# Where 64 row multiplies of the last adaLN gate stand among the two products of an MLP

## The chip, the cores and the metric

The kernel runs on one core of a Trainium2 chip. The metric is the time of one execution on the device in microseconds (us), the median of several runs. A core has engines with a queue of instructions each, which they work off in order: TensorE (PE in the profile; PEld is its weight load), VectorE (DVE), ScalarE (ACT), GpSimd (POOL) and SyncE (SP). They wait for each other through semaphores. DMA transfers are issued from the queues of SP, ACT and POOL and run beside the engines.

## The reference

One decoder layer: attention beside a recurrence, then an MLP with squared ReLU. A conditioning vector c gives six adaLN vectors (shift, scale and gate of each half). Cut to what matters here:

```
c_act = silu(c)
mod = (c_act @ w_ada + b_ada).reshape(B, 6, D)
sh1, sc1, gt1, sh2, sc2, gt2 = [mod[:, j][:, None, :] for j in range(6)]
...
h = rmsnorm(x, g_norm_mlp) * (1.0 + sc2) + sh2
hid = square(relu(einsum('bsd,df->bsf', h, w_mlp_in)))
y = einsum('bsf,fd->bsd', hid, w_mlp_out)
x = x + gt2 * y
return rmsnorm(x, g_norm_final)
```

There are 512 tokens, D is 2048 and the MLP is 8192 wide. gt2, the last gate, is needed only where the MLP's second product is finished.

## The kernel before

All values are float32. Each factor of a product is split into a high and a low half of TensorE's reduced format (a rounded copy on ScalarE, the rest by a subtraction on VectorE, `low`, L122), and a product is three matmuls.

**The two products of the MLP** are computed by Strassen's scheme: 7 products of sums of blocks in place of 8. One *set* is what one step along the inner dimension costs: 7 products, 2 halves and 3 matmuls each, 42 matmuls of 128x256. `operands` (L1053) makes a set's weights: one load of 512 KB into `raw` (three buffers), sums on VectorE (L1060, L1067, L1068), two copies on ScalarE (L1066, L1072) and two subtractions on VectorE (L122). `strassen` (L1083) runs over the sets of a list, holds its 7 results in 7 of the 8 PSUM banks, and calls `tick()` after each set.

The first product (loop at L1217) has 15 such groups of 8 sets, g = 1 to 15. After a group `combine` (L1110) adds up the 7 banks: a copy on ScalarE (L1113), then seven steps on VectorE (L1114 to L1120). The next group takes the eighth bank first and then the banks as combine frees them. `keep_parts` (L928) then squares and splits the result, adds sums for the second product (L948), and stores them as *parts* and *sums*; `hold_parts` (L952) does so for the last two groups without storing them.

The second product (loop at L1257) goes through a list `parts` of 13 pieces of 8, 16 or 12 sets; piece i works on column block n. Where a block isn't finished in a piece, its 7 banks are stored to DRAM (`prodD`, POOL's queue) and fetched again later: five by `load_pre` (L1236) on POOL's queue into tiles of the tag `n` (five buffers), two more on ACT's queue, copied into the banks by ScalarE at L1090 and L1092. Piece 3 (block 3) has 16 sets; the piece behind it is the first that fetches. Pairs of stored parts are fetched by `load_pair` (L1136: three loads at L1141, two at L1144, on SP's queue) and split by `split_pair` (L1148), both at set numbers worked out beforehand. From its block's last piece on, a block is added up with the gate: the first time at piece 9.

**The row multiplies.** `ada_late(GT2)` (L1188) computes gt2: 64 rows, each a load of 256 KB of `w_adaT` on SP's queue (L1192), three rows ahead, and one multiply with accumulation on VectorE (L1203); after four rows two small steps (L1208, L1209) give one column of gt2. It is a generator in the lane `bg2`: it yields a number of sets, and `tick()` runs it on when so many have passed. `pace[0]` is that number (1.9, L1215). `ensure(GT2)` (L1276) runs what is left of it, before piece 9's combine.

**What sets the order.** A scheduler orders each engine's instructions when the kernel is built, by the program's order less an offset given by `high_priority` (operands 200, combine 330 instructions ahead), and by when it takes data to be there. `keep_in_program_order` ties an instruction behind the one traced just before it on its engine. The rows' loads are tied in this way, their multiplies are not.

Sets are numbered below as VectorE begins them (its L1060): 1 to 120 are the first product, 121 to 244 the second; piece 3 has the sets 145 to 160.

Of the kernel before, what the change touches and what calls it, by code (L numbers as in the profile page):

```python
# [39 lines left out]
SH1, SC1, GT1, SH2, SC2, GT2 = range(6)  # L40
# [24 lines left out]
def hybrid_layer_kernel(  # L65
# [32 lines left out]
    def T(tag, dt=F32, cols=None):  # L98
        return new(next(split_tag) if tag == "w4" else tag, dt, cols)

    def new(tag, dt=F32, cols=None):
        count[0] += 1
        pool, bufs = (sp, BUFS[tag]) if tag in BUFS else pools[tag][:2]
        return pool.tile([P, cols or COLS[tag]], dt, tag=tag, name=f"{tag}_{count[0]}", bufs=bufs)

    def bank(tag):
        count[0] += 1
        return pp.tile([P, S], F32, tag=tag, name=f"ps_{tag}_{count[0]}", bufs=PBUFS[tag])
# [5 lines left out]
    stt = nc.vector.scalar_tensor_tensor  # L114
# [33 lines left out]
    def col(base, j):  # L148
        return vec[:, base + j : base + j + 1]
# [23 lines left out]
    for i in range(2):  # L173
        v = slice(i * S, (i + 1) * S)
        ps = bank("mm")
# [7 lines left out]
    def mod(m, j):  # L183
        return mods[:, m * NK + j : m * NK + j + 1]
# [80 lines left out]
    def blk(o):  # L265
        return slice(o * P, (o + 1) * P)


    class Lane:
# [8 lines left out]
        def next(self):  # L278
            if not self.queue:
                return False  # L280
            try:
                self.wait += next(self.queue[0]) or 0.0
            except StopIteration:
                self.queue.pop(0)
            return True
# [13 lines left out]
    bg, bgl, bg2 = Lane(), Lane(), Lane()  # L299

    def tick(dt=1.0):
        for lane in (bg, bgl, bg2):
            lane.run(dt)
# [137 lines left out]
    for o in range(8):  # L441
        t = T("a")
# [266 lines left out]
    pace = [3.2]  # L709

    def ensure(m):
        while m not in ready:
            assert bg2.next()
# [339 lines left out]
    def operands(src):  # L1053

        with tc.high_priority(offset=SETW):

            r = T("raw")
            nc.sync.dma_start(r.rearrange("p (c f) -> p c f", c=2), src)
            t = T("ts")
            tt(  # L1060
                out=t[:, : 2 * HT].rearrange("p (a b) -> p a b", a=2),
                in0=r[:, HT : 3 * HT].rearrange("p (a b) -> p a b", a=2),
                in1=r[:, q_(0)].unsqueeze(1).broadcast_to([P, 2, HT]), op=ALU.add,
            )
            h, lo = T("w3", F32R), T("w3", F32R)
            act(h, r[:, HT:], AF.Copy)  # L1066
            tt(out=t[:, q_(2)], in0=t[:, q_(0)], in1=r[:, q_(2)], op=ALU.add)  # L1067
            tt(out=t[:, q_(3)], in0=t[:, q_(2)], in1=r[:, q_(3)], op=ALU.add)  # L1068
            low(lo, r[:, HT:], h)
            out = {n: (h[:, q_(i)], lo[:, q_(i)]) for i, n in enumerate(("11", "22", "21"))}  # L1070
            h, lo = T("w4", F32R), T("w4", F32R)
            act(h, t, AF.Copy)  # L1072
            low(lo, t, h)
            for i, n in enumerate(("t1", "t3", "t2", "t4")):
                out[n] = h[:, q_(i)], lo[:, q_(i)]
        return out
# [3 lines left out]

    loaded = [None]

    def strassen(src, acts, after=None, pre=None, before=None, js=range(8)):  # L1083

        bs = [bank(next(turn)) for _ in PRODUCTS]
        if pre:
            n, ts = pre
            with tc.high_priority(offset=SETE):
                for b, t in zip(bs, ts):
                    act(b, t, AF.Copy)  # L1090
                for b, t in zip(bs[5:], load_pre(n, (5, 6), nc.scalar)):
                    act(b, t, AF.Copy)  # L1092
        if before:
            loaded[0] = before()
        for j in js:
            w, a = operands(src(j)), acts(j)
            for b, (an, wn) in zip(bs, PRODUCTS):
                (ah, al), (wh, wl) = a[an], w[wn]
                for i in range(2):
                    out, st = b[:, q_(i)], j == js[0] and i == 0 and not pre  # L1100
                    kw = dict(skip_group_check=True)
                    mm(out, wh[:, blk(i)], ah, start=st, stop=False, **kw)  # L1102
                    mm(out, wh[:, blk(i)], al, start=False, stop=False, **kw)  # L1103
                    mm(out, wl[:, blk(i)], ah, start=False, stop=j == js[-1], **kw)  # L1104
            if after:
                after(j)
            tick()
        return bs
# [71 lines left out]
    at = itertools.count(-8)  # L1180

    def after_set():
        for f, p in todo.get(next(at), []):
            f(p)

    LEAD, row = 3, ["n"]

    def ada_late(m):  # L1188

        def load(i):  # L1190
            t = T(row[0])
            tc.keep_in_program_order(nc.sync.dma_start(t, w_adaT[(m * NK + i // 4) * P : (m * NK + i // 4 + 1) * P, i % 4 * S : (i % 4 + 1) * S]))  # L1192
            return t

        ts = [load(i) for i in range(LEAD)]
        for i in range(4 * NK):
            t, q = ts.pop(0), i % 4
            if i + LEAD < 4 * NK:
                ts.append(load(i + LEAD))
            yield pace[0]  # L1200
            if q == 0:
                ga = T("ga")
            stt(  # L1203
                out=t, in0=t, scalar=1.0, in1=cb[q // 2][:, q % 2 * S : (q % 2 + 1) * S], op0=ALU.mult, op1=ALU.mult,
                accum_out=ga[:, q : q + 1],
            )
            if q == 3:
                tt(out=ga[:, :2], in0=ga[:, :2], in1=ga[:, 2:4], op=ALU.add)  # L1208
                stt(  # L1209
                    out=mod(m, i // 4), in0=ga[:, 0:1], scalar=ga[:, 1:2], in1=col(C_BADA, m * NK + i // 4),  # L1210
                    op0=ALU.add, op1=ALU.add,
                )
        ready.add(m)

    pace[0] = 1.9  # L1215
    w_pair = w_mlp_in.rearrange("(c k p) f -> k p c f", c=2, p=P)
    for g in range(1, NG):  # L1217
        if g == 2:
# [2 lines left out]
        bs = strassen(lambda j: w_pair[j][:, :, g * 512 : (g + 1) * 512], acts_in, last, js=range(KP)[:: -1 if g == 1 else 1])  # L1221
# [5 lines left out]
        bg.add((keep_parts if g < NG - 2 else hold_parts)(g, *rs))  # L1227


    row[0] = "a"  # L1230
    prodD = [[dp.tile([P, S], F32, name=f"prod_{n}_{i}") for i in range(7)] for n in range(NO)]
    w_blocks = w_mlp_out.rearrange("(g c b p) d -> g b p c d", c=2, b=2, p=P)
    x2 = {}
# [2 lines left out]
    def load_pre(n, js, queue=nc.gpsimd):  # L1236
        ts = [T("n") for _ in js]
        for t, j in zip(ts, js):
            queue.dma_start(t, prodD[n][j])
        return ts  # L1240
# [9 lines left out]
    nxt = None  # L1250
# [6 lines left out]
    for i, (n, ps) in enumerate(parts):  # L1257
        seen = {m for m, _ in parts[: i + 1]}
        left = [m for m, _ in parts[i + 1 :]]

        def before():
            if left and left[0] in seen:
                return left[0], load_pre(left[0], range(5))

        def after(p, n=n, early=(ps[4],) if n not in left and n < NO - 1 else ()):
            after_set()
            if p in early:
                load_x2(range(n * 4, n * 4 + 4), x1D)
            if i == len(parts) - 1 and p == ps[5]:
                load_x2(range(12, NK), x1D)  # L1270

        src = lambda q: w_blocks[ORDER[q] // 2][ORDER[q] % 2][:, :, n * 512 : (n + 1) * 512]
        bs = strassen(src, acts_out, after, nxt, before, ps)
        nxt = loaded[0]
        if n not in left:
            ensure(GT2)  # L1276
            cs = [T("cb"), T("cb")]
            qs = [t[:, j * S : (j + 1) * S] for t in cs for j in range(2)]
            with tc.high_priority(offset=SETE):
                qs = combine(bs, *qs)  # L1280
            if n == NO - 1:
                for q, d in zip(qs, yD):
                    nc.gpsimd.dma_start(d, q)
                continue
            if acc2 is None:
                acc2 = T("a")
            with tc.high_priority(offset=SETW):
                for k, tok, q in quarters(n, *qs):
                    t = x2[k][:, tok]
                    stt(out=t, in0=q, scalar=mod(GT2, k), in1=t, op0=ALU.mult, op1=ALU.add)  # L1290
                for k, q in zip(range(n * 4, n * 4 + 4), qs):
                    add_square(acc2, x2[k], q, k == 0)
                    if n == 0:
                        nc.gpsimd.dma_start(x2D[k], x2[k])
        else:
            with tc.high_priority(offset=SETE):
                for j, b in enumerate(bs):
                    t = T("a")
                    copy(j + 1, t, b)
                    nc.gpsimd.dma_start(prodD[n][j], t)  # L1300
# [12 lines left out]
    for p in final:  # L1313
        t = T("a", F32R)
# [154 lines left out]
```

## Time and profile before

| | |
|---|---|
| runs, median (lowest to highest) | 1995.27 us (1991.86 to 1996.58), 3 runs |
| profiled execution | 1994.49 us |
| its span in the profile | 1992.7 us |
| granted TensorE clock, mean | 0.996 |
| row multiplies (L1203), first and last start | 832.6 and 1408.0 us |
| rows' multiply, mean length | 0.68 us, 64 times |
| second product's weights (512 KB), issue to landing | 4.6 us, median of 124 |

Times are us from the span's start. A row of the timeline gives start, length, engine, line, instruction, output and inputs, and in brackets how long the engine stood idle before it and for whom. A row of waits gives who waited for whom: us in all, how often, the longest. In a table of stretches a column holds an engine's busy us and, in brackets, its instructions; then TensorE's clock, the DMA engines' share and GB/s.

### The profile page before, as it was taken

The numbers are of one execution on the slowest core, as the hardware profiler recorded it, in microseconds if no ns is written. First come the engines' busy times: TensorE is split into PE (matmuls) and PEld (weight loads), VectorE is DVE, ScalarE is ACT, GpSimd is POOL, SyncE is SP. The second block draws the span as 40 slices with busy tenths as digits, with TensorE's granted clock in tenths as the row PEclk, the third lists the DMA queues.
The fourth block names the chain that finished last, engine by engine and source line by source line (L and its number), as shares of the span: only waits on it lengthen the run. The fifth ranks groups of instructions, "written<-read, shape, count | busy, mean of one in ns | idle before, by whom it ended". The sixth has DMA issues, their size and how long they took to land. (4 is left out here: it accounts for less than half of the span.)

```text
span 1992.7 us, 37203 instructions
## 1 busy us (share of the span) xinstructions
PE 1941.9 (97%) x14148; PEld 1815.3 (91%) x14148; DVE 1760.6 (88%) x2979; ACT 1074.6 (54%) x1580; POOL 193.6 (10%) x307
## 2 busy tenths in 40 slices
PE   8999999999999998999999999999999999999997
PEld 6787887788888998999999999999999999999996
DVE  8998776988998599999999999999879779879996
ACT  5443564786433385555555555556445555556552
POOL 0000000000000000112111211200110210211100
PEclk9999999999999999999999999999999999999998
DMA  9896655556779544766666665755567668679653
GB/s 368 304 340 198 212 163 185 179 163 218 226 251 365 170 134 129 239 194 213 221 196 203 226 197 190 232 173 210 185 241 262 238 249 278 220 253 341 225 197 112
DMA packets 205238, 443.51 MB, mean 223 GB/s; under 512 B 20481, under 2 KB 42113, under 8 KB 205058
## 3 DMA queue, kind: packets, MB, share of 16 engines
q1 hardware_dynamic: 176338, 356.58, 54.2%
q0 software_dynamic: 23680, 77.61, 10.5%
q10 hardware_dynamic: 5040, 6.93, 1.0%
q8 instruction: 111, 1.82, 0.4%
q14 instruction: 69, 0.57, 0.1%
HBM read 376.30 MB, written 64.75 MB: 221 GB/s over the span
## 5 line engine op out<-in xcount | busy, mean ns | idle before, releaser
L1102 PE MATMUL ps_mm<-a,w 128*128 128x256 f32 x1696 | 469.1, 277 | 3.0 <-DVE a L1114 1.2
L1104 PE MATMUL ps_mm<-a,w 128*128 128x256 f32 x1696 | 469.2, 277 | 0.4 <-DVE w L122 0.3
L1103 PE MATMUL ps_mm<-a,w 128*128 128x256 f32 x1696 | 469.1, 277 | 0.4 <-DVE a L122 0.3
L1072 ACT ACTIVATE w<-ts 128x1024 fp32r<-128x1024 f32 x244 | 258.4, 1059 | 273.1 <-DVE ts L1068 241.5
L1104 PE MATMUL ps_z<-a,w 128*128 128x256 f32 x1304 | 362.0, 278 | 6.9 <-DVE w L122 6.8
L1102 PE MATMUL ps_z<-a,w 128*128 128x256 f32 x1304 | 362.2, 278 | 3.4 <-DVE a L1118 1.6
L1103 PE MATMUL ps_z<-a,w 128*128 128x256 f32 x1304 | 361.4, 277 | 0.1
L122 DVE TENSOR_TENSOR w<-ts,w 128x1024 fp32r<-128x1024 f32 x244 | 297.8, 1221 | 55.4 <-PE ps_mm L1103 20.4
L1102 PEld LDWEIGHTS ps_mm<-a,w 128*128 128x128 f32 x1696 | 318.4, 188 | 4.3 <-issue 2.5
L1104 PEld LDWEIGHTS ps_mm<-a,w 128*128 128x128 f32 x1696 | 318.7, 188 | 1.1 <-DVE w L122 1.0
L1103 PEld LDWEIGHTS ps_mm<-a,w 128*128 128x128 f32 x1696 | 318.7, 188 | 0.8 <-DVE a L122 0.8
L122 DVE TENSOR_TENSOR w<-raw,w 128x768 fp32r<-128x768 f32 (+1 forms) x296 | 267.5, 905 | 37.8 <-ACT w L244 24.0
L1066 ACT ACTIVATE w<-raw 128x768 fp32r<-128x768 f32 x244 | 204.5, 839 | 174.8 <-issue 80.5
L1104 PEld LDWEIGHTS ps_z<-a,w 128*128 128x128 f32 x1304 | 245.6, 189 | 8.2 <-DVE w L122 8.1
L1102 PEld LDWEIGHTS ps_z<-a,w 128*128 128x128 f32 x1304 | 245.8, 188 | 4.9 <-issue 2.1
L1103 PEld LDWEIGHTS ps_z<-a,w 128*128 128x128 f32 x1304 | 245.7, 188 | 0.6 <-DVE a L122 0.6
L244 ACT ACTIVATE wh<-wr 128x512 fp32r<-128x512 f32 (+1 forms) x184 | 113.2, 618 | 142.4 <-PE ps_mm L262 61.8
L1060 DVE TENSOR_TENSOR ts<-raw 128x512 f32<-128x512 f32 x244 | 166.8, 684 | 14.2 <-DMA raw<-in_w_mlp_out_dram 13.4
L259 PE MATMUL ps_mm<-a,wh 128*128 128x512 f32 x448 | 176.8, 395 | 2.6 <-DVE a L460 1.0
L263 PE MATMUL ps_mm<-a,wl 128*128 128x512 f32 x448 | 175.0, 391 | 1.5 <-DVE wl L122 1.3
L262 PE MATMUL ps_mm<-a,wh 128*128 128x512 f32 x448 | 174.9, 390 | 0.0
L211 DVE SCALAR_TENSOR_TENSOR x<-x,cb 128x1024 f32<-128x1024 f32 x108 | 131.2, 1218 | 23.4 <-DMA x<-in_w_adaT_dram 23.3
(336 smaller groups left out, 4007.7 us busy)
## 6 DMA issues: line engine op xcount, KB each, us to landing
raw<-in_w_mlp_out_dram SPq DMA_DIRECT2D x124, 512.0 KB, 4.6
raw<-in_w_mlp_in_dram SPq DMA_DIRECT2D x120, 512.0 KB, 3.8
x<-in_w_adaT_dram SPq DMA_DIRECT2D x108, 512.0 KB, 5.6
wr<-in_w_in_dram SPq DMA_DIRECT2D x160, 256.0 KB, 3.4
tt<-in_w_adaT_dram SPq DMA_DIRECT2D x52, 512.0 KB, 6.2
part<-a POOLq DMA_DIRECT2D x84, 256.0 KB, 3.9
a<-part SPq DMA_DIRECT2D x84, 256.0 KB, 6.3
prod<-a POOLq DMA_DIRECT2D x63, 256.0 KB, 5.8
```

Of the source, the lines that this page charges most:

```text
L122: tt(out=out, in0=full, in1=f32(high), op=ALU.subtract)
L211: ins = stt(out=t, in0=t, scalar=1.0, in1=cb[q_], op0=ALU.mult, op1=ALU.mult, accum_out=self.ga[:, q_ : q_ + 1],)
L244: act(h[:, :n], r[:, :n], AF.Copy)
L259: first = mm(out, wh, ah, start=start, stop=False, **kw)
L262: mm(out, wh, al, start=False, stop=False, **kw)
L263: mm(out, wl, ah, start=False, stop=stop, **kw)
L1060: tt(out=t[:, : 2 * HT].rearrange("p (a b) -> p a b", a=2), in0=r[:, HT : 3 * HT].rearrange("p (a b) -> p a b", a=2), in1=r[:, q_(0)].unsq ...
L1066: act(h, r[:, HT:], AF.Copy)
L1072: act(h, t, AF.Copy)
L1102: mm(out, wh[:, blk(i)], ah, start=st, stop=False, **kw)
L1103: mm(out, wh[:, blk(i)], al, start=False, stop=False, **kw)
L1104: mm(out, wl[:, blk(i)], ah, start=False, stop=j == js[-1], **kw)
```

## The change

It does five things:
- the pace of the 64 rows becomes 2.7 sets in the first product and 1.3 in the second (1.9 in both before); at the passage 5.0 sets are added to the wait once;
- the rows' tiles always come from the tag `n` (in the second product they came from `a`);
- the rows' multiplies are tied to their place in the program, as their loads are;
- `strassen` can call its `before` at a later set (`at`); piece 3 does so at its 13th set, so that the partial products for piece 4 are asked for there and not at its first set;
- `ensure(GT2)` stands in that `before`, ahead of `load_pre`, so all rows are done before the partial products take the `n` tiles.

```diff
-    def strassen(src, acts, after=None, pre=None, before=None, js=range(8)):
+    def strassen(src, acts, after=None, pre=None, before=None, js=range(8), at=0):
...
-        if before:
-            loaded[0] = before()
-        for j in js:
+        for n_, j in enumerate(js):
+            if before and n_ == at:
+                loaded[0] = before()
...
-    LEAD, row = 3, ["n"]
+    LEAD, ROWS = 3, (2.7, 1.3)
...
-            t = T(row[0])
+            t = T("n")
...
-            stt(
+            ins = stt(
...
+            tc.keep_in_program_order(ins)
...
-    pace[0] = 1.9
+    pace[0] = ROWS[0]
...
-    row[0] = "a"
+    pace[0] = ROWS[1]
+    bg2.wait += 5.0
...
             if left and left[0] in seen:
+                ensure(GT2)
                 return left[0], load_pre(left[0], range(5))
...
-        bs = strassen(src, acts_out, after, nxt, before, ps)
+        bs = strassen(src, acts_out, after, nxt, before, ps, 12 if i == 3 else 0)
...
-            ensure(GT2)
```

**VectorE ahead of combine, sets 25 and 26** (the first group boundaries with rows). `n_...,ga_...` is a row, `w_...` the last steps of a set's weights, L1114 combine's first step. Before:

```order
L1203 SCALAR_TENSOR_TENSOR n_8770,ga_9286<-n_8770,cb_81 128x512
L122 TENSOR_TENSOR w_1804_9081<-ts_9072,w_1803_9080 128x1024
L122 TENSOR_TENSOR w_1820_9155<-raw_9150,w_1819_9154 128x768
L1060 TENSOR_TENSOR ts_9224<-raw_9222 128x512
L1209 SCALAR_TENSOR_TENSOR mods<-ga_8768,vec 128x1
L1067 TENSOR_TENSOR ts_9224<-ts_9224,raw_9222 128x256
L1203 SCALAR_TENSOR_TENSOR n_8891,ga_9286<-n_8891,cb_81 128x512
L1068 TENSOR_TENSOR ts_9224<-ts_9224,raw_9222 128x256
L1203 SCALAR_TENSOR_TENSOR n_9010,ga_9286<-n_9010,cb_82 128x512
L122 TENSOR_TENSOR w_1822_9161<-ts_9152,w_1821_9160 128x1024
L122 TENSOR_TENSOR w_1830_9227<-raw_9222,w_1829_9226 128x768
L1114 TENSOR_TENSOR a_9133<-ps_o_8626,a_9131 128x512
```

In the change, at the same place:

```order
L1060 TENSOR_TENSOR ts_9141<-raw_9139 128x512
L1067 TENSOR_TENSOR ts_9141<-ts_9141,raw_9139 128x256
L1068 TENSOR_TENSOR ts_9141<-ts_9141,raw_9139 128x256
L122 TENSOR_TENSOR w_1802_9075<-ts_9066,w_1801_9074 128x1024
L122 TENSOR_TENSOR w_1817_9144<-raw_9139,w_1816_9143 128x768
L1060 TENSOR_TENSOR ts_9216<-raw_9214 128x512
L1067 TENSOR_TENSOR ts_9216<-ts_9216,raw_9214 128x256
L1068 TENSOR_TENSOR ts_9216<-ts_9216,raw_9214 128x256
L122 TENSOR_TENSOR w_1819_9150<-ts_9141,w_1818_9149 128x1024
L122 TENSOR_TENSOR w_1828_9219<-raw_9214,w_1827_9218 128x768
L1114 TENSOR_TENSOR a_9122<-ps_o_8618,a_9120 128x512
```

The three rows and the small step ahead of combine are gone from here. By groups (8 sets from a combine to the next), rows in before and in the change: sets 10 to 17: 2 and 1; 18 to 25: 7 and 4; 26 to 33: 8 and 3; then 4 or 5 and 3 in each of the ten groups up to 113; 114 to 121: 1 and 3. Behind set 121 there are 4 rows in before, the last at set 134, and 23 in the change, at sets 129 to 157.

**SP's queue at the passage**, between the weights of sets 122 and 123 (L1058 loads weights, L1141 and L1144 a pair, L1192 a row). Before:

```order
L1141 DMA a_15189<-part_6139 128x512
L1141 DMA a_15190<-part_6139 128x512
L1141 DMA a_15191<-part_6139 128x512
L1144 DMA a_15195<-sum_6155 128x512
L1144 DMA a_15196<-sum_6155 128x512
L1192 DMA n_15205<-in_w_adaT_dram 128x512
L1141 DMA a_15263<-part_6139 128x512
L1141 DMA a_15264<-part_6139 128x512
L1141 DMA a_15265<-part_6139 128x512
L1144 DMA a_15269<-sum_6155 128x512
L1144 DMA a_15270<-sum_6155 128x512
L1058 DMA raw_15613<-in_w_mlp_out_dram 128x2x512
```

In the change:

```order
L1141 DMA a_15129<-part_6139 128x512
L1141 DMA a_15130<-part_6139 128x512
L1141 DMA a_15131<-part_6139 128x512
L1144 DMA a_15135<-sum_6155 128x512
L1144 DMA a_15136<-sum_6155 128x512
L1058 DMA raw_15542<-in_w_mlp_out_dram 128x2x512
```

The second pair and the row now follow behind the weights of set 123.

**ScalarE around the copy of the first partial product** (L1090), in piece 3. Before, between the weights of sets 148 and 149:

```order
L1066 ACTIVATE w_2964_17174<-raw_17170 128x768
L1072 ACTIVATE w_2966_17180<-ts_17172 128x1024
L1090 ACTIVATE ps_mm_18027<-n_16972 128x512
L1239 DMA n_18039<-prod_5_15433 128x512
L1066 ACTIVATE w_2970_17230<-raw_17226 128x768
```

In the change, between those of sets 152 and 153:

```order
L1151 ACTIVATE a_17397<-a_17068 128x512
L1151 ACTIVATE a_17400<-a_17069 128x512
L1151 ACTIVATE a_17459<-a_17138 128x512
L1151 ACTIVATE a_17462<-a_17139 128x512
L1090 ACTIVATE ps_mm_18027<-n_17760 128x512
L1066 ACTIVATE w_3008_17481<-raw_17477 128x768
L1072 ACTIVATE w_3010_17487<-ts_17479 128x1024
```

The copy stands four sets later, behind four conversions of split_pair (L1151). The load it waits for takes the buffer of the 60th row, whose multiply is at set 152 on VectorE.

## The prediction, made before the changed kernel was run

> **What bounds the kernel now.** I read the busy times first, then busy time by stretch, then TensorE's list of waits, then single stretches of the timeline.
>
> ```profile
> PE 1941.9 (97%) x14148; PEld 1815.3 (91%) x14148; DVE 1760.6 (88%) x2979; ACT 1074.6 (54%) x1580; POOL 193.6 (10%) x307
> ```
>
> TensorE is the bound as a whole, VectorE follows at 88%. Where TensorE loses time must be read by stretch (columns: length, then busy us and count of PE, PEld, DVE, ACT, POOL; clock; DMA share; GB/s):
>
> ```profile
> 850.00:947.00 97.00, 94.36 (x812) 92.71 (x811) 96.04 (x174) 54.04 (x74) 18.41 (x27) 1.00 0.64 204
> 947.00:1348.00 401.00, 398.77 (x3503) 397.68 (x3502) 394.55 (x672) 221.19 (x293) 66.18 (x97) 1.00 0.64 206
> 1348.00:1400.00 52.00, 49.35 (x417) 48.02 (x416) 50.50 (x81) 32.33 (x47) 3.76 (x7) 1.00 0.58 201
> 1400.00:1830.00 430.00, 430.00 (x3797) 430.00 (x3796) 358.61 (x529) 230.06 (x302) 51.38 (x95) 1.00 0.71 252
> 1830.00:1952.00 122.00, 120.58 (x1041) 118.72 (x1039) 108.56 (x171) 65.51 (x93) 18.44 (x34) 1.00 0.64 212
> ```
>
> From 1400 to 1830 TensorE never stops: 430 / 3797 = 0.1133 us a matmul, so a set of 42 takes 4.76 us and a group of 8 sets 38.07 us. At that pace the matmuls of the other four stretches need 92.0, 396.7, 47.2 and 117.9 us; TensorE loses 5.0, 4.3, 4.8 and 4.1 us there. In the first three of them VectorE is busy 96 to 99% of the time; in the stretch without loss only 83%. So the first product stands at the edge of two engines. The waits between 850 and 1400 name the place:
>
> ```profile
> PE ps_z L1102 <- DVE a L1118: 1.6, 3, 0.5
> PE ps_mm L1102 <- DVE a L1114: 1.2, 1, 1.2
> PE ps_z L1102 <- ACT a L1113: 1.0, 1, 1.0
> ```
>
> L1113 to L1120 are combine, which reads a finished group's banks; the next group may not write a bank before. TensorE waits at the group boundaries, for a VectorE that comes to combine late.
>
> **What a row and a group cost on VectorE.** Its timeline ahead of one boundary (start, length, instruction):
>
> ```profile
> 1269.53 0.68 DVE L1060 TENSOR_TENSOR ts<-raw 128x512 f32<-128x512 f32 x1
> 1270.13 0.68 DVE L1203 SCALAR_TENSOR_TENSOR n<-n,cb 128x512 f32<-128x512 f32 x1
> 1270.74 0.08 DVE L1203 DVE_READ_ACCUMULATOR n<-n,cb 128x1 f32 x1
> 1270.74 0.42 DVE L1067 TENSOR_TENSOR ts<-ts,raw 128x256 f32<-128x256 f32 x1
> 1271.07 0.15 DVE L1208 TENSOR_TENSOR ga<-ga 128x2 f32<-128x2 f32 x1
> 1271.19 0.43 DVE L1068 TENSOR_TENSOR ts<-ts,raw 128x256 f32<-128x256 f32 x1
> 1271.54 0.21 DVE L1209 SCALAR_TENSOR_TENSOR mods<-ga,vec 128x1 f32<-128x1 f32 x1
> 1271.67 1.22 DVE L122 TENSOR_TENSOR w<-ts,w 128x1024 fp32r<-128x1024 f32 x1
> 1272.80 0.95 DVE L122 TENSOR_TENSOR w<-raw,w 128x768 fp32r<-128x768 f32 x1
> 1273.67 0.68 DVE L1114 TENSOR_TENSOR a<-ps_mm,a 128x512 f32<-128x512 f32 x1
> ```
>
> Lengths overlap, so I take starts: a row (L1203) holds VectorE for 0.61 us, its two small steps once in four rows for 0.12 + 0.13, a 128x512 step 0.60. A set's own five steps take 0.60 + 0.33 + 0.35 + 1.13 + 0.87 = 3.28. A group in the steady state is 8 x 3.28 = 26.24, plus 14 steps of 128x512 (7 of combine, 3 of L122, 4 of L948) = 8.4, so 34.64, plus rows. I count rows by group in the order of instructions, by sets on VectorE (set 1 is the first of group 1):
> - Sets 18 to 25 and 26 to 33 hold 7 and 8 rows in before, 4 and 3 in the change. With the small steps (and two more 0.60 steps in the first, one of them gone in the change) that is 40.4 and 40.0 us against 38.07, an excess of 2.4 and 1.9, which is most of the 5.0 lost. With the change 37.9 and 36.7: no excess.
> - The ten groups from set 34 to 113 hold 4 or 5 rows in before (37.3 to 37.9 us), 3 in the change (36.4 to 37.3). There VectorE fits, but with 0.2 to 0.8 us to spare, out of which it also waits for rows' loads:
>
> ```profile
> DVE n L1203 <- DMA n<-in_w_adaT_dram: 2.5, 6, 0.8
> ```
>
> These six waits come from multiplies hoisted to where their load only just lands; the change keeps a multiply at its place, 8 sets (38 us) after its load, so they go.
>
> **First term, first product.** Of the 5.0 I take 4.4 (0.6 stays: the boundary near 850, with the same steps before it). Of the 4.3 I take 3.4: the spare time doubles, but the three rows of a group now stand in the last sets before its boundary, as the scheduler had put most of the four. Bounds 1.0 (only the 2.5 us of load waits, in part) and 4.3. Sum -7.8.
>
> **Second term, the passage between the products.**
>
> ```profile
> 1338.34 1.29 SPq L1141 DMA_DIRECT2D a<-part  x3
> ...
> 1345.36 0.42 SPq L1058 DMA_DIRECT2D raw<-in_w_mlp_out_dram  x1
> ```
> ```profile
> 1351.87 0.69 DVE L1060 TENSOR_TENSOR ts<-raw 128x512 f32<-128x512 f32 x1 [1.11 <-DMA raw<-in_w_mlp_out_dram]
> ```
> ```profile
> 1351.88 0.84 ACT L1066 ACTIVATE w<-raw 128x768 fp32r<-128x768 f32 x1 [1.97 <-DMA raw<-in_w_mlp_out_dram]
> 1352.63 0.58 ACT L1113 ACTIVATE a<-ps_z 128x512 f32<-128x512 f32 x1
> ```
>
> The weights of set 123 are issued at 1345.36, behind ten loads of pairs and a row on SP's queue; ScalarE waits 1.97 us for them with combine's first copy (L1113) queued behind, VectorE waits 1.11, and TensorE then stands twice (the 1.0 and the 1.2 above). In the change five of those loads and the row stand behind the weights, which frees them some 3 us earlier than they were wanted late. Against it the change puts three rows instead of one into sets 114 to 121, +1.2 us. Of the 4.8 lost I take -2.0 (bounds 0 and -4.3); the rest is hold_parts with VectorE full, and what is late next is its L122.
>
> **Third term, part 3.** The 23 rows behind set 121 (4 in before) lie in sets 129 to 157. Up to 152 VectorE has 3.3 to 5.1 us of work a set and mostly below 4.76, so they hide in its idle time. From 153 the pairs are split too: counted like a group, sets 153 to 159 come to 35.3 us against 7 x 4.76 = 33.3, 2.0 over. VectorE's cushion there, from its last step for a set to that set's first matmul:
>
> ```profile
> 1480.39 1.23 DVE L122 TENSOR_TENSOR w<-ts,w 128x1024 fp32r<-128x1024 f32 x1 [1.14 <-PE ps_mm L1103]
> 1484.40 0.69 DVE L1060 TENSOR_TENSOR ts<-raw 128x512 f32<-128x512 f32 x1 [1.21 <-DMA raw<-in_w_mlp_out_dram]
> 1489.98 0.69 DVE L1060 TENSOR_TENSOR ts<-raw 128x512 f32<-128x512 f32 x1 [1.97 <-DMA raw<-in_w_mlp_out_dram]
> 1502.71 1.22 DVE L122 TENSOR_TENSOR w<-ts,w 128x1024 fp32r<-128x1024 f32 x1
> ```
> ```profile
> 1484.99 0.28 PE L1102 MATMUL ps_mm<-a,w 128*128 128x256 f32 x1
> ...
> 1504.03 0.28 PE L1102 MATMUL ps_mm<-a,w 128*128 128x256 f32 x1
> ```
>
> It is 1484.99 - 1481.62 = 3.4 us at set 148 and 0.1 at set 152, used up by late weights (1.21 and 1.97) while partial products and pairs were loaded together, and by this:
>
> ```profile
> 1480.28 0.60 ACT L1090 ACTIVATE ps_mm<-n 128x512 f32<-128x512 f32 x1 [3.55 <-DMA n<-prod]
> ```
> ```profile
> 1473.10 0.55 POOL L1239 DMA_DIRECT2D n<-prod  x1
> ```
> ```profile
> 1472.00:1511.00 39.00, 39.00 (x347) 39.00 (x346) 32.42 (x49) 19.82 (x27) 3.79 (x7) 1.00 1.04 386
> ```
>
> ScalarE stands 3.55 us in front of the copy of a partial product, issued 7.2 us before. In the change that load waits until the 60th row has freed its buffer, at set 152, and the copy stands just behind; queued behind it on ScalarE are the weights of set 153, for which VectorE and then TensorE wait. The stall thus moves from set 148, where the cushion was full, to 152; I take 2.5 us, from 0 (the four conversions now ahead of the copy hide it) to 7.2. The late weights at 150 and 151 should shrink, since the partial products have left that place; I leave 1 us of them. So 3.4 - 1 - 2.5 - 2.0 = -2.1, and some of it is taken up since the second product of a set wants its weights later than the first: +1.3, bounds 0 and 9.
>
> ```profile
> raw<-in_w_mlp_out_dram SPq DMA_DIRECT2D x124, 512.0 KB, 4.6
> a<-part SPq DMA_DIRECT2D x84, 256.0 KB, 6.3
> ```
>
> With 12 weights of 0.52 MB, 40 pair loads, 7 stores, 6 partial products and 5 rows of 0.26 MB, the 57 us of 12 sets have 21.5 MB to move: 55.7 us at 386 GB/s. It just fits.
>
> [...]
>
> **Sum.** -7.8 - 2.0 + 1.3 = -8.5 against the profiled execution, 1994.49 (span 1992.7 and 1.8 around it): 1986.0. The median shown is 0.8 higher, so I write **1986.5**.
>
> **Rivals.**
> - *The boundaries stay.* Combine's own seven steps set the small gaps after 947, not VectorE's backlog: for it, they vary from 0 to 0.9 with the same number of rows; against it, each ends on a step of combine that starts late. Then -4.4 - 1.0 - 1.0 + 1.3 = -5.1: 1990.
> - *Given back.* The first term holds, but in part 3 the weights are late as before (cushion 0.1 at set 152) and VectorE's 2.0 and ScalarE's 3.55 come on top: +5.5, and nothing is won between the products: -7.8 + 5.5 = -2.3, 1992 to 1994.
> - *Slower.* ScalarE waits in front of the partial product (place: set 152) for as long as the weights of set 151 took, from their issue at 1478.53 (row below) to the 1489.98 above, 11.4 us. With VectorE's 2.0 less a cushion of 3.4 TensorE stands for 10.0 us. Such a stand at one place has a second price:
>
> ```profile
> 1478.53 0.63 SPq L1058 DMA_DIRECT2D raw<-in_w_mlp_out_dram  x1
> ```
> ```profile
> 779.58 0.58 PE L1104 MATMUL ps_z<-a,w 128*128 128x256 f32 x1 [4.18 <-DVE w L122]
> 779.96 0.42 PE L1102 MATMUL ps_z<-a,w 128*128 128x256 f32 x1
> 780.17 0.42 PE L1103 MATMUL ps_z<-a,w 128*128 128x256 f32 x1
> ```
>
>   After a wait of 4.18 us matmuls start 0.21 us apart instead of 0.113; should that last 4 us, it costs 2 more. Together +12.0, with -7.8 and the passage's 0: +4.2, 1999. It decides from about 8 us of ScalarE's wait. [...]
> - *Does nothing*: the order shows the rows moved, so only where gains and losses cancel.
>
> **How the numbers follow.** Forecast 0.6 (1981 to 1988.5), boundaries stay 0.17 (1988.5 to 1991.3), given back 0.15 (of it 0.14 within 0.2%), slower 0.08. The range is 1981.0, from the bounds 5.0 + 4.3 + 4.3 = 13.6, to 1993.5, which leaves the slower rival and the end of the third outside. What a measurement of this kernel can tell from no change is about 0.2%, 4 us: faster 0.78, same 0.14, slower 0.08.
>
> **What would show it.** In the profile of the change: losses at 850 to 947 near 0.6, at 947 to 1348 below 1.5, at the passage near 2.8; no L1203 waiting for its load before 1350; weights of set 123 landed before VectorE wants them. In part 3 a few TensorE waits for L122 around sets 153 to 159, 1 to 2 us in all, and ScalarE's wait before L1090 at set 152, not 148. A loss in part 3 above 5 us, or small boundary waits as frequent as before, would make it wrong.

## The result, and the profile after

The changed kernel takes 1985.38 us (median of 6 runs) against 1995.10 (6 runs of before); the ratio is 0.9947, with a 95% interval of 0.9935 to 0.9959. One of the six runs of the change took 3251.8 us at a mean granted clock of 0.557; the ratio leaves it out, and the other five have a median of 1983.61. The forecast was 1986.5. The profiled execution has a span of 1981.3 us, against 1992.7.

The profile of the change, busy times, then busy time by stretch (columns as in the prediction), then TensorE's waits from 850 to 1400 (us in all, times, longest):

```profile
PE 1936.3 (98%) x14148; PEld 1813.5 (92%) x14148; DVE 1760.7 (89%) x2979; ACT 1077.1 (54%) x1580; POOL 193.4 (10%) x307
```
```profile
850.00:947.00 97.00, 97.00 (x858) 97.00 (x858) 96.04 (x162) 55.66 (x73) 19.75 (x29) 1.00 0.66 210
947.00:1348.00 401.00, 400.50 (x3532) 400.13 (x3531) 392.96 (x649) 225.63 (x299) 64.54 (x95) 1.00 0.64 204
1348.00:1400.00 52.00, 51.50 (x441) 50.64 (x440) 51.77 (x87) 31.18 (x45) 3.76 (x7) 1.00 0.54 183
1400.00:1830.00 430.00, 429.49 (x3786) 429.09 (x3786) 369.12 (x574) 234.47 (x311) 56.35 (x104) 1.00 0.74 263
```
```profile
PE ps_mm L1102 <- DVE a L1114: 0.5, 1, 0.5
PE ps_mm L1103 <- DVE a L122: 0.3, 1, 0.3
```

VectorE does the same work (1760.7 us, 1760.6 before) and is still busy 98 to 100% of the time up to 1400, but TensorE loses nothing from 850 to 947: 858 matmuls stand there instead of 812. Of eleven rows of waits two are left.

The whole program is now some 10 us earlier, so stretches of equal times no longer hold the same sets. From here on I count by sets: the time from one set's first matmul to another's (a set taken as 42 matmuls in TensorE's order), less 4.76 us a set, is what TensorE lost. In us:

```
sets      before  change | e1   e2   e3   e4   e5   e6   e7   e9   e10  e11
1-16       11.91  11.76 | 12.75 13.23 12.21 12.63 12.64 11.26 11.16 12.11 11.19 11.23
17-33       5.17   0.00 |  1.10  2.69  0.00  0.00  4.76  0.00  0.00  5.04  5.12  0.00
34-113      4.26   0.01 |  3.39  0.06  0.01  0.01  3.72  0.01  0.01  3.63  2.46  0.01
114-121     2.82   1.08 |  7.40  1.90  1.27  1.20  6.01  0.69  1.04  2.96  0.60  0.27
122-144     2.23   2.30 |  2.98  2.10  2.30  4.61  2.30  2.32  2.33  2.43  2.41  2.16
145-160     0.00   0.00 |  0.00  5.07  0.00  0.00  0.00  0.00  0.44  0.00  0.00  0.00
161-224     1.01   1.11 |  1.05  1.14  2.61  1.26  1.12  1.06  2.67  1.03  1.53  1.34
225-244     3.00   3.34 |  3.39  3.15  2.94  2.92  3.50  3.04  2.98  2.86  3.00  3.06
```

The change gains 5.17 in sets 17 to 33, 4.25 in 34 to 113, 1.74 in 114 to 121, and elsewhere it differs by less than 0.4: 10.8 us between the MLP's first and last matmul, which is what the ratio says (10.6). Up to set 14 every kernel here runs the same program, and still the MLP began anywhere from 754.8 to 759.8 us and sets 1 to 16 lost from 11.2 to 13.2; a span's difference of a few us says little, a group's loss says more.

**Why the boundaries are free now.** Call VectorE's *lead* the time from the end of a set's first L122 (128x1024) to where TensorE wants it, 0.68 us (six matmuls) behind the set's first matmul. Around the boundary of sets 105 and 106, in the change:

```profile
1260.49 1.23 DVE L122 TENSOR_TENSOR w<-ts,w 128x1024 fp32r<-128x1024 f32 x1
...
1267.62 1.21 DVE L122 TENSOR_TENSOR w<-ts,w 128x1024 fp32r<-128x1024 f32 x1
```
```profile
1265.09 0.28 PE L1102 MATMUL ps_mm<-a,w 128*128 128x256 f32 x1
...
1269.85 0.28 PE L1102 MATMUL ps_mm<-a,w 128*128 128x256 f32 x1
```

The lead is 1265.09 + 0.68 - 1261.72 = 4.05 at set 105 and 1269.85 + 0.68 - 1268.83 = 1.70 at 106: combine takes 2.4 us of it. In before the same two sets have 1.40 (from the rows at 1271.67 in the prediction, with the set's first matmul at 1273.61) and -0.05:

```profile
1278.80 1.21 DVE L122 TENSOR_TENSOR w<-ts,w 128x1024 fp32r<-128x1024 f32 x1
```
```profile
1279.28 0.28 PE L1102 MATMUL ps_mm<-a,w 128*128 128x256 f32 x1
```

1.40 - 2.4 leaves -1.0, and TensorE loses 0.92 there. So the lead is a stock. It is full at 4.06 us, where VectorE waits for TensorE's matmuls instead (the row at 1482.83 in the account of part 3 shows such a wait). A boundary draws 2.4 us from it, the sets between put it back, and over a whole group it gains 38.07 less VectorE's work. In before the sets 18 to 33 emptied it, and 37.3 to 37.9 us of work gained only 0.2 to 0.8 a group, some of it spent again on waits; in the change 36.7 gains 1.4, and the stock is full or nearly so (3.9 to 4.06) ahead of every boundary from set 41 on.

### The profile page after: what moved, and what is told of

Its sections match the earlier page's. It is cut to its first block, busy times and chain, and to the rows that moved or that the text cites. A ratio compares the mean times of both kernels' runs of the same rounds, so it can differ in the third digit from the quotient of the medians.

```text
span 1981.3 us, 37180 instructions
## 1 busy us (share of the span) xinstructions
PE 1936.3 (98%) x14148; PEld 1813.5 (92%) x14148; DVE 1760.7 (89%) x2979; ACT 1077.1 (54%) x1580; POOL 193.4 (10%) x307
## 3 DMA queue, kind: packets, MB, share of 16 engines
q0 software_dynamic: 23680, 77.61, 10.6%
## 4 chain that ended last, share of the span: by engine, by line
PE 53%; DVE 3%; DMA 1%; issue 1%; ACT 1%; POOL 0%; DVEq 0%; POOLq 0%; ACTq 0%; SPq 0%
PE ps_mm L1104 9%; PE ps_mm L1102 9%; PE ps_mm L1103 9%; PE ps_z L1103 7%; PE ps_z L1104 7%; PE ps_z L1102 7%; PE ps_o L1104 2%; PE ps_o L1102 2%; PE ps_o L1103 2%; DVE w L122 1%; DVE ts L1060 0%; DMA a<-sum 0%; DMA a<-part 0%; DVE a L1357 0%; DVE a L122 0%
## 5 line engine op out<-in xcount | busy, mean ns | idle before, releaser
L122 DVE TENSOR_TENSOR w<-ts,w 128x1024 fp32r<-128x1024 f32 x244 | 297.7, 1220 | 52.9 <-PE ps_mm L1103 16.7
L122 DVE TENSOR_TENSOR w<-raw,w 128x768 fp32r<-128x768 f32 (+1 forms) x296 | 267.2, 904 | 41.1 <-ACT w L244 24.9
L122 DVE TENSOR_TENSOR wl<-wr,wh 128x512 fp32r<-128x512 f32 (+1 forms) x184 | 123.5, 673 | 30.5 <-ACT wh L244 30.2
```

The lines of the kernel that those rows point to most:

```text
L122: tt(out=out, in0=full, in1=f32(high), op=ALU.subtract)
```

## The experiments

Every kernel but e7 computes the same as the kernel it comes from; e7 adds five steps whose result nobody uses. Medians and, where there is one, the ratio to before with its interval:

| | us | ratio |
|---|---|---|
| e1 tie alone | 1993.93 | 0.9990 (0.9974 to 1.0006) |
| e2 paces without the tie | 1991.67 | 0.9982 (0.9969 to 0.9996) |
| e3 part 3 arranged as before | 1984.98 | 0.9945 (0.9925 to 0.9965) |
| e4 no wait between the products | 1987.52, one run | |
| e5 before, one pair later | 1998.25, one run | |
| e6 change, one pair earlier | 1982.78, one run | |
| e7 five more steps | 1985.58, one run | |
| e8, e11 clear passage | 1980.79, 1982.22 | 0.9924 (0.9901 to 0.9946), 0.9942 (0.9921 to 0.9962) |
| e9 before, last four rows tied | 1993.72, one run | |
| e10 e9 and one pair later | 1989.67, one run | |
| e12 the change again | 1985.05 | 0.9950 (0.9932 to 0.9968) |

### Number of rows, or their place: e1 and e2

e1 is before with the tie alone, e2 the change without it:

```diff
 # e1, on before
-            stt(
+            ins = stt(
...
+            tc.keep_in_program_order(ins)
 # e2, on the change
-            tc.keep_in_program_order(ins)
```

> The kernel before, with one part of the change: the row multiplies tied to their place; pace 1.9, tags and load_pre as before. By the order of VectorE's instructions sets 18 to 25 and 26 to 33 then hold 5 and 5 rows (7 and 8 in before, 4 and 3 in the change), the ten groups up to set 113 still 4 or 5. Theory A, the number of rows in a group decides: sets 17 to 33 lose 1.1 us (39.1 and 38.1 us of VectorE's work against 38.07 a group) in place of 5.2, and sets 34 to 113 lose 4.3 as before; with the passage as before the time is 4 us under before, about 1991. Theory B, what decides are multiplies that the scheduler had put where their load just lands, and close ahead of combine: sets 34 to 113 lose under 1 us, and the time is 7 to 8 us under before, about 1987.

> The change without the tie of the row multiplies. The scheduler then puts 8 rows into sets 18 to 25 (five of them at sets 25 and 26), 4 into the next group, 3 into each up to set 113. Theory A (number of rows in a group): sets 17 to 33 lose 2.4 us (40.4 us of work in the first group, 37.4 in the second), sets 34 to 113 under 0.5; about 3 us over the change. Theory B (place of the rows): sets 34 to 113 still lose 2 us or more from waits for rows' loads and late combines, and the time is 5 us or more over the change.

Sets 17 to 33 lost 1.10 in e1 (1.1 expected) and 2.69 in e2 (2.4 expected): the excess of VectorE's work over 38.07 us a group is what is lost. Sets 34 to 113 lost 3.39 in e1, where no row waits for its load, and 0.06 in e2, where the scheduler still put the rows ahead of combine: **the number of rows decides, not their place** (theory A). (How much of it is lost varies: 3.63 and 2.46 in e9 and e10, which are before up to there.)

But neither time came out as theory A had it, for places that I had not counted on. Without the tie, part 3 lost 5.07 us. VectorE's waits of e2 from 1340 to 1520, one of them in its timeline, and TensorE's from 1455 to 1510:

```profile
DVE n L1203 <- DMA n<-in_w_adaT_dram: 14.1, 5, 5.3
```
```profile
1477.79 0.69 DVE L1203 SCALAR_TENSOR_TENSOR n<-n,cb 128x512 f32<-128x512 f32 x1 [5.34 <-DMA n<-in_w_adaT_dram]
```
```profile
PE ps_o L1104 <- DVE w L122: 2.5, 3, 1.9
```

At 1.3 sets a row, the scheduler puts untied multiplies close behind their loads: for the five that wait, SP issued the load only some 2 to 5 us before the wait began, and 5.3 to 7.3 us before the multiply could start; up to 5.3 us of the lead go in one wait. With the tie no L1203 waits at all in the change, where the same loads are issued 24 us or more ahead of their multiplies. And with the tie at the old pace (e1) the passage lost 7.40: VectorE came there with a lead of 0.9, TensorE waited 3.0 us for a set's L122, and then combine stood behind late weights:

```profile
1352.75 0.69 DVE L1060 TENSOR_TENSOR ts<-raw 128x512 f32<-128x512 f32 x1 [1.79 <-DMA raw<-in_w_mlp_out_dram]
...
1354.28 0.69 DVE L1114 TENSOR_TENSOR a<-ps_mm,a 128x512 f32<-128x512 f32 x1
```

So the two halves of the change only pay together: by the ratios 2.0 (not clear of nothing) and 3.6 us alone, 10.6 both.

### Part 3: e3 and e7

e3 puts the second product back as it was; e7 adds work on VectorE there:

```diff
 # e3, on the change
-            t = T("n")
+            t = T(row[0])
...
+    row[0] = "a"
...
-                ensure(GT2)
                 return left[0], load_pre(left[0], range(5))
...
-        bs = strassen(src, acts_out, after, nxt, before, ps, 12 if i == 3 else 0)
+        bs = strassen(src, acts_out, after, nxt, before, ps)
...
         if n not in left:
+            ensure(GT2)
 # e7, on the change, behind the tied multiply
+            for _ in range(1 if i >= 59 else 0):
+                tc.keep_in_program_order(tt(out=t, in0=t, in1=t, op=ALU.add))
```

> The change with the second product's arrangement of before: partial products asked for at piece 3's first set, rows in tiles of the tag a, ensure ahead of piece 9's combine; paces, the 5.0 sets and the tie stay. First product and passage lose what they lose in the change (1.1 us in sets 114 to 121, 2.3 in 122 to 144). Theory 1, the cushion of 4 us on VectorE hides what part 3 brings wherever the partial products stand: sets 145 to 160 lose under 0.3 us and the time is that of the change. Theory 2, the later partial products are what keeps part 3 free: weights at sets 150 to 152 are late by about 3 us again, the cushion at set 152 (0.8 us in before) is overdrawn by the rows at sets 150 to 152 (1.8 us) and again by those at 155 to 158, and sets 145 to 160 lose 1 to 3 us.

> The change with one more 128x512 step on VectorE (0.60 us, a sum of the row's tile with itself, used by nobody) behind each of the last five row multiplies, 3.0 us in all at sets 152 to 158. In the change VectorE's lead there, from the end of a set's last high-by-low step to where TensorE wants it, falls from 4.06 us to 1.1 at set 158 and is refilled by set 161. If that lead is all that hides part 3's work, sets 145 to 160 lose 3.0 - 1.1 = 1.9 us at most, 1.3 if the fifth step comes too late to count. If something else covers it: under 0.3. By the prediction's own sum, in which the lead was used up, about 3.

In e3 sets 145 to 160 lost nothing (theory 1), though the lead went down to 0.14 at set 159; 1.2 us were lost in set 161, where TensorE waited 0.9 for a copy of a partial product (L1092). In e7 the lead went to -0.36 at set 159, and just there TensorE lost 0.44; of the 3.0 us only about 1.2 had come by set 158, where the change is lowest, and the rest fell where the lead refills, so 1.9 was too much. It lost 1.4 more in set 161, at L1092:

```profile
PE ps_mm L1102 <- ACT ps_mm L1092: 1.0, 1, 1.0
```

Both say that the lead alone covers sets 145 to 160, to the last half microsecond. The late copies in set 161 go back to the lead too, as far as the traces show it (no run tried it alone). The lead there was 2.62 in e3 and 2.48 in e7 instead of 4.06; ScalarE, just ahead of its copies, waited 1.5 and 1.6 us for VectorE's sums (L1068), and it issued the load for the last L1092 only 0.8 and 0.6 us ahead of TensorE's slot 161, against 2.3 in the change. ScalarE in e3, with slot 161 at 1537.15:

```profile
1534.17 1.06 ACT L1072 ACTIVATE w<-ts 128x1024 fp32r<-128x1024 f32 x1 [1.48 <-DVE ts L1068]
...
1536.38 0.33 ACTq L1242 DMA_DIRECT2D n<-prod  x1
...
1541.64 0.60 ACT L1092 ACTIVATE ps_mm<-n 128x512 f32<-128x512 f32 x1 [0.86 <-DMA n<-prod]
```

With a ratio of 0.9945 against 0.9947, the three edits that e3 takes back (the tag, the later partial products, the earlier `ensure`) earn nothing that can be measured.

### The passage: e5, e6, e9, e10

My prediction put the passage's gain down to SP's queue, where the weights of set 123 no longer stand behind the second pair. e5 moves that pair behind them in before, e6 moves it ahead of them in the change; e9 and e10 tie only the last four rows of before, without and with the moved pair:

```diff
 # e5 and e10, on before
-            todo.setdefault(use - 7 - q % 8 + q % 8 * 3 // 2, []).append((load_pair, p))
+            todo.setdefault(use - 7 - q % 8 + q % 8 * 3 // 2 + (q == 3), []).append((load_pair, p))
 # e6, on the change
+            todo.setdefault(use - 7 - q % 8 + q % 8 * 3 // 2 - (q == 3), []).append((load_pair, p))
 # e9 and e10, on before, behind the multiply
+            if i >= 60:
+                tc.keep_in_program_order(ins)
```

> The kernel before with one due number changed: the second pair of the passage is asked for one set later, so that on SP's queue the weights of set 123 stand ahead of it (behind one pair and the row) instead of behind it. Rows as in before. If SP's order is what the passage gained in the change: sets 114 to 121 lose 1.1 to 1.5 us in place of 2.8 and VectorE's wait of 1.1 us for these weights is gone. If it is what the change did to VectorE's rows: still 2.5 to 3. All else as in before: 5.2 in sets 17 to 33, 4.3 in 34 to 113, nothing in 145 to 160.

> The change with the second pair of the passage asked for one set earlier: on SP's queue both pairs then stand ahead of the weights of set 123, as in before (the row behind them). Rows as in the change. If SP's order decides: sets 114 to 121 lose 2 to 3 us in place of 1.1, with a wait of VectorE for these weights ahead of combine. If the rows decide: 1.1 as in the change. All else as in the change.

Both expectations failed in both directions: 6.01 with the pair moved, 0.69 with it put back. VectorE's timeline ahead of combine (L1114) in e5:

```profile
1351.38 0.68 DVE L1060 TENSOR_TENSOR ts<-raw 128x512 f32<-128x512 f32 x1
1353.40 0.69 DVE L1203 SCALAR_TENSOR_TENSOR n<-n,cb 128x512 f32<-128x512 f32 x1 [1.33 <-DMA n<-in_w_adaT_dram]
...
1355.95 0.68 DVE L1114 TENSOR_TENSOR a<-ps_mm,a 128x512 f32<-128x512 f32 x1
```

The weights are in time now, and it is the untied row that waits 1.33 us for its load, with combine behind it. That gave theory M, on which e9 and e10 were made:

> The kernel before with only the last four row multiplies tied to their place: the two that stood on VectorE ahead of the last combine (sets 122 and 123) then come at sets 130 and 131; SP's queue, weights of set 123 behind two pairs and a row, stays. Theory M: the passage's loss follows the start of combine's first step (L1114), put off by whatever waits ahead of it on VectorE: here the late weights alone (1.1 us), not the row (0.6), so L1114 starts 3.0 us behind TensorE's start of that set in place of 3.6, and sets 114 to 121 lose 2.2 us in place of 2.8. Theory R: the rows alone decide: 1.1 as in the change. Theory S: SP's order alone decides: 2.8.

> The same tie of the last four row multiplies, and the second pair asked for one set later, so that the weights of set 123 stand ahead of it on SP's queue. By theory M neither late weights nor a row stand ahead of combine: L1114 starts 1.3 us behind TensorE's start of that set, and sets 114 to 121 lose 0.5 to 1.0 us, against 2.8 in before and 6.0 with the pair moved alone, where the untied row waited 1.3 us for its load ahead of combine. Theory R: as the run with the tie alone. Theory S: about 1.1 here, but then the pair moved alone should have given that too.

The same place in e9 and in e10:

```profile
1351.29 0.69 DVE L1060 TENSOR_TENSOR ts<-raw 128x512 f32<-128x512 f32 x1 [2.24 <-DMA raw<-in_w_mlp_out_dram]
...
1353.96 0.68 DVE L1114 TENSOR_TENSOR a<-ps_mm,a 128x512 f32<-128x512 f32 x1
```
```profile
1346.90 0.69 DVE L1060 TENSOR_TENSOR ts<-raw 128x512 f32<-128x512 f32 x1
...
1349.56 0.68 DVE L1114 TENSOR_TENSOR a<-ps_mm,a 128x512 f32<-128x512 f32 x1
```

Against TensorE's start of slot 121 in each run, L1114 starts 3.60 us later in before, 4.26 in e5, 3.74 in e9, 1.97 in the change, 1.59 in e6, 1.38 in e10, 0.84 earlier in e11; the losses are 2.82, 6.01, 2.96, 1.08, 0.69, 0.60 and 0.27, in the same order (e5's has a second part, in the last section). e1, which has such a second part too, fits (7.98 and 7.40); e2 does not (0.73 and 1.89): there a set's L122 stands between combine's steps, and TensorE waits for a later one of them, L1118. Two things may stand unlanded ahead of combine, the weights of set 123 and a row; taking away one leaves the other (e5, e9), taking away both gives 0.60 (e10). In e9 the weights landed 0.6 us later than in before, so the row's going won nothing and the loss was 2.96, not 2.2.

For e6, SP's queue of that run, and of the change, at the weights of set 123:

```profile
1333.36 0.38 SPq L1058 DMA_DIRECT2D raw<-in_w_mlp_out_dram  x1
```
```profile
1331.24 0.38 SPq L1058 DMA_DIRECT2D raw<-in_w_mlp_out_dram  x1
```

TensorE starts slot 121 at 1341.48 and 1341.25 there, at 1351.42 in before: the weights are issued 8.1, 10.0 and (1345.36) 6.1 us ahead of it. In e6 the pair stands ahead of them as in before, but SP came to the first pair 14.8 us ahead (1326.72) and not 13.1 (1338.34), and the row's load stands behind. SP waits for a free `raw` there, which VectorE gives back (in the change 17.6 us in all for its L122 from 1310 to 1350), and VectorE's lead at set 119 was 2.20 (2.07 in the change) instead of 1.19. That this is what brought SP forward was read from the traces, not tried by itself.

### The passage cleared: e4, e8, e11 and e12

```diff
 # e4, on the change
-    bg2.wait += 5.0
 # e8 and e11, on the change (with e5's moved pair)
     for g in range(1, NG):
...
+        pace[0] = 2.7 if g < 5 else 2.3
+        if g == 14:
+            bg2.wait += 13
```

> The change without the 5.0 sets of wait between the products. Four rows then stand in sets 126 to 130, none behind set 152. If VectorE's work by groups decides, sets 122 to 137 hold 77.8 us of it against 76.1 (75.2 in the change), so sets 122 to 144 lose up to 1.7 us more than the 2.3 of the change; if the rows only fill idle time there, nothing more. In sets 145 to 160 nothing is lost either way, and the cushion at set 158 is 3 us or more in place of 1.1.

> A variant of the change: pace 2.7 up to group 4 and 2.3 from there (3 or 4 rows a group), no row between sets 106 and 130 but one at set 121, and the second pair of the passage behind the weights of set 123; 23 rows at sets 130 to 157. Sets 17 to 113 lose under 0.2 us as in the change if groups of up to 37.3 us of VectorE's work refill its lead; the passage has 38.8 us in sets 122 to 129 in place of 41.8, so sets 114 to 144 lose 1.5 to 2.5 us in place of 3.4; sets 145 to 160 nothing. The time is 1 to 2 us under the change, 1984. If the passage's loss comes from combine and hold_parts alone, it is that of the change.

> The variant with a clear passage once more, beside the change on the same chip. By the losses counted in its profile it gains 0.95 us in sets 114 to 144 on the change and nothing elsewhere, so its ratio to before should be 0.0005 below that of the change, too little to be told apart; its lower time in the first look came from 3.5 us ahead of the MLP, where both programs are the same, and should not come again.

> The change once more, beside the variant with a clear passage: 0.9947 of before as the first time, within 0.001; losses by groups of sets as the first time within 0.2 us from set 17 on.

Without the 5.0 sets, rows stand among hold_parts' steps, and sets 122 to 144 lost 4.61, 2.3 more than the change (1.7 expected). With the passage cleared, sets 114 to 144 lost 2.43 in place of 3.38, in e8 and in e11 alike. That 0.95 us is the same in both profiles, but the times cannot tell the variant from the change: 0.9924 and 0.9942 against 0.9947 and 0.9950, with intervals that overlap. e8's shorter span came from ahead of the MLP, as thought: the MLP began at 754.8 us in e8, at 759.2 in e11 and at 755.9 in e12. e12's losses were those of the change within 0.1 us in sets 16 to 160, but 2.38 in sets 161 to 224 in place of 1.11, the same kernel: there a difference of 1 us means nothing (in e3 and e7 it was at sets 161 to 168, where all other runs lost 0).

## Why the prediction was right, and where it was not

- **First product**: -7.8 forecast, -9.4 measured. The arithmetic by groups (excess over 38.07) held in three kernels. The term was mis-sized because I left 1.5 us at the boundaries, not having seen that a group with room refills the lead. The step that failed is "out of which it also waits for rows' loads", taken as part of the loss: without those six waits the loss stays (e1, 3.39 of 4.26, where kernels that are the same as before up to there lost 2.46 to 4.26). The rival "the boundaries stay" fell with 0.01.
- **Passage**: -2.0 forecast, -1.7 measured, for a reason that was half wrong. Late weights with combine behind them on VectorE were the trouble, and in before itself SP's order cures them (e10). But in the change "five of those loads and the row stand behind the weights, which frees them" was not needed (e6); and I had not seen that the untied row was as dangerous as the weights (e5). "Three rows instead of one into sets 114 to 121, +1.2 us" cost TensorE nothing, but only because the lead paid: from set 114 to 121 it rises by 2.26 in before (-0.05 to 2.21) and by 0.6 in the change (1.55 to 2.15), which came to set 114 with 1.6 more.
- **Part 3**: +1.3 forecast, 0 measured; the place was right, three sizes were not. ScalarE's stall and what it waits for (POOL waits for the 60th row):

```profile
1488.66 0.60 ACT L1090 ACTIVATE ps_mm<-n 128x512 f32<-128x512 f32 x1 [2.65 <-DMA n<-prod]
```
```profile
1481.67 0.55 POOL L1241 DMA_DIRECT2D n<-prod  x1 [20.60 <-DVE n L1203]
```

2.65 us, against 2.5 taken, at set 152 as forecast. The lead at sets 151 and 158, and between them VectorE's only wait:

```profile
1482.83 1.23 DVE L122 TENSOR_TENSOR w<-ts,w 128x1024 fp32r<-128x1024 f32 x1 [0.53 <-PE ps_mm L1103]
...
1490.06 0.96 DVE L122 TENSOR_TENSOR w<-raw,w 128x768 fp32r<-128x768 f32 x1 [0.93 <-ACT w L1066]
...
1519.08 1.21 DVE L122 TENSOR_TENSOR w<-ts,w 128x1024 fp32r<-128x1024 f32 x1
```
```profile
1487.43 0.28 PE L1102 MATMUL ps_mm<-a,w 128*128 128x256 f32 x1
...
1520.75 0.28 PE L1102 MATMUL ps_mm<-a,w 128*128 128x256 f32 x1
```

It falls from 4.05 to 1.14. The cushion was 4.06 and not 3.4, since I had measured to a set's first matmul and not to the one that needs the data; of the 2.9 that went, the stall took 0.93 (the wait at 1490.06) and not 2.5, so most of ScalarE's 2.65 us did not reach VectorE; VectorE's work took the other 2.0, as forecast (from 1484.06 to 1520.29, the ends of the first and the last of these VectorE rows, it needed 36.2 us, 35.3 without the wait, for 7 x 4.76 = 33.3); late weights took nothing and not 1. "Given back" and "slower" needed a lead below zero; it stayed 1.1 us above.
- **Sum**: -8.5 forecast, -10.8 measured in the MLP; the times say 0.53%, 10.6 us. The range held it. That the median of six came out 1.1 us from the forecast is in part luck: single runs of the change lie 7 us apart without the long one, and the terms were off by 1.6, 0.3 and 1.3. Three slips in the working change nothing: 1986.0 and 0.8 make 1986.8, not 1986.5; VectorE's shares in the three stretches are 97 to 99%; and the 386 GB/s that the 21.5 MB were set against are not the most that was moved: in e1 it was 399 GB/s from 1347.70 to 1351.00 and 408 from 1355.20 to 1357.50.

## What to carry to other kernels

Where two engines run at the same pace, measure the slower one's lead over the faster, to the instruction that needs the data: it is a stock that regular events draw from and spare time refills (here 4.06 us when full; a boundary drew 2.4, a group of 36.7 us put 1.4 back), and small waits can end with a few steps of work moved to a stage that has spare time (of TensorE's 15 waits from 850 to 1400 two were left with 19 of 64 rows moved). When such work is spread more thinly, tie it to its place if its loads share a queue with others; a scheduler that thinks a load has landed puts a wait in front of everything else (untied, five rows of e2 waited 14.1 us in all, up to 5.34 at once; tied, none waited). What stands ahead of a hand-over such as combine must have nothing unlanded in it (late weights took 1.11 us in before, a late row 1.33 in e5), and one late operand hides behind another, so cure them together before judging either (with one cured 6.01 and 2.96 us were lost, with both 0.60).

## What the hardware showed

TensorE's granted clock was 0.50 behind shorter waits than the 4.18 us of the prediction: 1.87 us in e2, 2.79 in e5 and 3.0 in e1 (0.52 there from 1351.0 to 1353.2). e2 and e5, TensorE's timeline at the wait and the stretch of half clock (the number behind POOL's is the granted clock):

```profile
1496.70 0.38 PE L1104 MATMUL ps_o<-a,w 128*128 128x256 f32 x1 [1.87 <-DVE w L122]
```
```profile
1498.10:1501.10 3.00, 3.00 (x17) 3.00 (x16) 3.00 (x7) 2.92 (x6) 0.55 (x1) 0.50 0.93 307
```
```profile
1356.78 0.55 PE L1102 MATMUL ps_mm<-a,w 128*128 128x256 f32 x1 [2.79 <-DVE a L1114]
```
```profile
1357.00:1362.00 5.00, 5.00 (x24) 5.00 (x25) 5.00 (x10) 3.80 (x7) 0.00 (x0) 0.50 0.71 232
```

In e2 TensorE stood 1.87 us (2.14 from matmul to matmul), worked at full pace for 1.3 us, and only then ran at half clock for 3.4; in e5 and e1 the matmuls behind waits of 2.8 and 3.0 us were slow at once. A gap of 1.96 us between matmuls in the change (from 770.10) and one of 1.89 in before (from 770.72) brought no half clock before the next wait, 4.11 and 4.18 us long (to 779.02 and 779.58); there it lasted 3.41 us in the change (779.18 to 782.59) and 6.83 in before (777.60 to 784.42). The 3.42 us ahead of the half clock in e2 and e5, and as long a stretch with the gap near 770 in the change, with TensorE's busy time first:

```profile
1494.58:1498.00 3.42, 1.55 (x14) 1.35 (x13) 3.39 (x7) 2.40 (x4) 0.55 (x1) 1.00 1.00 355
```
```profile
1352.24:1355.66 3.42, 1.75 (x13) 1.35 (x11) 2.23 (x5) 0.91 (x2) 0.00 (x0) 1.00 1.06 402
```
```profile
768.94:772.36 3.42, 1.74 (x15) 1.54 (x14) 3.42 (x8) 1.12 (x2) 0.00 (x0) 1.00 0.00 0
```

TensorE was idle for 55%, 49% and 49% of these stretches; behind the third the clock stayed full. What decides between them was not shown. In e5 half clock began at 1355.66, 1.1 us before the wait ended. In the prediction I had this second price only behind 4.18 us; in e5 it made 2.5 us of the 6.0 lost (25 matmuls 0.1 us late each: 24 in the 5.00 us above, where the 4.60 us from 1362.40 hold 42).
